# Branch A's background steps: 16 beside its first pair of heads, 10 beside each later one

## The chip, the cores and the metric

The kernel runs on one core of one Trainium2 chip. The metric is the device time of one execution in microseconds (us). The engines are named as the profile names them: PE is TensorE (PEld its weight loads), DVE is VectorE, ACT is ScalarE, POOL is GpSimd, SP is SyncE.

## The reference

One inference step of a trunk of two layers on 1152 tokens (128 of context, 1024 latent), 9 tiles of 128, with 1024 channels. Each layer projects the normed stream by one matrix and feeds three branches from it:

```python
def mixer_tail(x, gate, oa, g_a, ob, g_b, oc, g_c, merge, P):
    m = jax.nn.sigmoid(merge).reshape(B, T, N_BRANCH, D_MODEL)
    y = (m[:, :, 0] * ((oa * jax.nn.silu(g_a)) @ P['w_br_a'])
         + m[:, :, 1] * ((ob * jax.nn.silu(g_b)) @ P['w_br_b'])
         + m[:, :, 2] * ((oc * jax.nn.silu(g_c)) @ P['w_br_c']))
    return x + gate * (y @ P['w_out'])
```

Branch A (oa) is windowed attention of 8 heads with two key heads: each tile of 128 latent queries sees the context block, its own block and its two neighbours, with a sink in the softmax, normed and rotated q and k. Branch B (ob) is a gated linear recurrence over a convolution, branch C (oc) differential attention of 4 heads over all tokens. Each output is multiplied by its own silu gate, which is again a projection of the stream.

## The kernel before, in words

Nearly all matmuls split float32 operands in a high and a low half: `mm3` (L180 to L183) issues three matmuls, high by high, high by low and low by high. A projection of 384 columns over the 1024 channels is 8 times 3 = 24 matmuls of 128x384 into one PSUM bank of the ring ps_s, which has four. PSUM holds besides three banks ps_t (transposes) and one ps_o (outputs).

`unit_phase` does one layer's attention. In the foreground run the heads of branch C and then four pairs of heads of branch A (`g` = 0 to 3), each in five groups of tiles, GR = (0), (1, 2), (3, 4), (5, 6), (7, 8). For a group `q_conv` splits q, `a_probs` makes the scores on PE (L661, L662), adds the mask on DVE (L667, L664 for tile 0), takes exponentials on ACT (L676) and normalises; `flush` then runs the products of the group before (`a_pv`: transposes L701, the high half PT copied by ACT, the low half by DVE L93, products L710 into ps_o, which ACT and DVE copy out into Oa). Foreground code is under `fg`, which gives it a higher priority in the scheduler.

The background is a generator of steps, each one projection chunk of 24 matmuls with what reads it. For branch A 45 steps are left: 9 of `a_gemm2` (q of the later pairs: two tiles at a time through `qk_rows`, L378 to L420), then for each pair three gate chunks (`gate_silu`) and, behind the second to fourth gate and at the end, six steps of the recurrence's projections. `step(n)` takes n of them; the tables BGQ, BG0 and BGA say how many after each group. What is left after the last group runs behind the two last flushes. The order on each engine comes from a scheduler that takes these calls with their priorities.

Two pieces of it matter. `qk_rows` copies two tiles' chunks into `qkraw` (ACT), squares them into `qktmp` (ACT, L388), sums them (DVE, L389), takes an inverse root (DVE, many small `rsq`), multiplies (DVE), and lets POOL scale and rotate them (`qkraw`, `qktmp`, `aq`). `gate_silu` takes a tanh of each chunk (ACT, L449, tile `gt`) and multiplies by the chunk in PSUM (DVE, L102, tile `gate`), which frees the ps_s bank. `qkraw`, `qktmp` and `gt` share the ring D of three buffers in SBUF; RINGS lists the buffers of each ring (W holds weights: `wsraw`, `wsh`, `wsl`, the low half `wsl` made by POOL; T holds PT).

After branch A comes the tail, whose first matmuls write background-like chunks into ps_s and ps_o and start the recurrence (`luhl` into ps_t).

Of the kernel before, what the change touches and what calls it, by code (L numbers as in the profile page):

```python
# [38 lines left out]

BGQ = (2, 2, 2, 3, 2, 1)  # L40
BG0 = (6, 2, 2, 1, 1, 0)
BGA = (3, 2, 2, 2, 2, 2)

RINGS = {"S": 26, "P": 7, "T": 2, "Q": 2, "W": 7, "D": 3, "E": 2, "cx": 1, "tab": 1}

# [9 lines left out]
def hybrid_dit_kernel(ctx, tc, I, O):  # L55
# [30 lines left out]
    def dma(out, in_):  # L86
        nc.sync.dma_start(out=out, in_=in_)
# [262 lines left out]
    def load_wu(L, groups, early=False):  # L350

        src = I["w_in"][L.l].rearrange("(k p) n -> p k n", p=128)
        raws, w = [], []

        def conv(raw):
            m = raw.shape[1]
            hi, lo = al("W", "uwh", m, 384), al("W", "uwl", m, 384)
            split(hi, lo, raw, "A", "P")
            return [(hi[:, j, :], lo[:, j, :]) for j in range(m)]
        for k0 in (0, 3, 6):  # L360
            m = min(3, KT - k0)
            raw = al("W", "wuraw", m, 384)
            for g, c0 in enumerate(groups):
                dma(raw[:, :, 128 * g:128 * g + 128], src[:, k0:k0 + m, c0:c0 + 128])
            raws.append(raw)
            if not early:
                w += conv(raws.pop())
        for raw in raws:
            w += conv(raw)
        return w  # L370
# [72 lines left out]
    def gate_silu(L, c0, put):  # L443

        gate = al("S", "gate", NTOK)

        def f(c, p):
            t = al("D", "gt", 384)
            A.activation(out=t, in_=p, func=AF.Tanh, scale=0.5)  # L449
            stt(gate[:, c * 384:(c + 1) * 384], t, 1.0, p, ALU.add, ALU.mult)  # L450
        hi, lo = ws_load(w_in_cols(L.l, c0), KT)
        put(gate)
        for c in range(3):
            f(c, ws_chunk(L, hi, lo, c))
            yield
# [5 lines left out]
    def c_groups(h):  # L461
        return [CQC + 128 * h, CKC + 128 * h, CVC + 128 * h]

    def qkv_gemm(L, u, w, gains, okey, oval, eng=None):

        u.q, u.kr, u.vr = al("S", "uq", 9, 2, 64), al("S", "ukr", 9, 2, 64), al("S", "uvr", 9, 128)
        for i0 in range(0, 9, 3):
            pss = []
            for t in range(3):
                p = tok_gemm(L, i0 + t, w)  # L470
                acopy(u.vr[:, i0 + t, :], p[:, 256:384])
                pss.append(p)
                if t < 2:
                    yield
            ii = slice(i0, i0 + 3)
            qk_rows(L, i0, pss, gains, [u.q[:, ii, :, :], u.kr[:, ii, :, :]], eng)
            if i0 == 0:
                dma(okey, u.kr[:, 0, :, :])
                dma(oval, u.vr[:, 0, :])
            yield  # L480
# [148 lines left out]
    def a_gemm2(L):  # L629
        u, w = L.ua, L.wu2  # L630
        u.qs = [u.q] + [al("S", "aq", 9, 2, 64) for _ in range(3)]
        for i0 in range(0, 9, 2):
            n = min(2, 9 - i0)
            pss = []
            for t in range(n):
                pss.append(tok_gemm(L, i0 + t, w))
                if t < n - 1:
                    yield
            qk_rows(L, i0, pss, (2, 2, 2), [u.qs[g][:, i0:i0 + n, :, :] for g in (1, 2, 3)])
            yield  # L640
# [86 lines left out]
    def unit_phase(L):  # L727

        l = L.l
        a_groups = [CQA, CKA, CVA]  # L730
        pend = None

        done = None

        def flush():
            nonlocal pend, done
            d, done = done, None
            if pend:
                pend()
                pend = None  # L740
            if d:
                d()

        def start(h):
            u = Unit()
            if h < 4:
                L.units.append(u)
                return qkv_gemm(L, u, L.wu, (0, 1), O["nck"][0, l, :, h, :, :], O["ncv"][0, l, :, h, :],
                                V if h == 0 else None)
            L.ua = u  # L750
            return qkv_gemm(L, u, L.wu, (2, 3), O["nak"][0, l], O["nav"][0, l].rearrange("t v d -> t (v d)"))

        def background():

            for h in range(4):
                L.wu = load_wu(L, c_groups(h + 1) if h < 3 else a_groups)
                yield from start(h + 1)
                yield from gate_silu(L, CGC + 128 * h, lambda gate, u=L.units[h]: setattr(u, "gate", gate))
            L.wu2 = load_wu(L, [CQA + 128, CQA + 256, CQA + 384])
            yield from a_gemm2(L)  # L760
            for g in range(4):
                yield from gate_silu(L, CGA + 128 * g, L.gates.append)
                if g:
                    yield from lru_x(L, g - 1)
            yield from lru_x(L, 3)

        def step(n):
            for _ in range(n):
                next(bg, None)

        def fg(f, *args):
            with tc.high_priority(offset=HPO):
                return f(*args)
        for _ in start(0):
            pass
        bg = background()
        step(BG0[0])
        fg(c_kconv, L, L.units[0], 0)
        for h in range(4):
            u = L.units[h]  # L780
            u.l0 = tl("l0", 9, bufs=2)
            qn = BGQ if h else BG0
            if h:
                step(qn[0])
            fg(v_conv, u, I["cache_c_v"][0, l, :, h, :])
            for g, tiles in enumerate(GR):
                n = len(tiles)
                q = fg(q_conv, u.q[:, tiles[0]:tiles[0] + n, :, :].rearrange("p t m d -> p (t m) d"), 2 * n)
                Ps = [fg(c_probs, L, u, tiles[0], q, 0)]
                fg(flush)  # L790
                if n == 2:
                    Ps.append(fg(c_probs, L, u, tiles[1], q, 1))

                def pend(u=u, tiles=tiles, Ps=Ps, h=h, g=g):
                    if g == 0:
                        u.o = al("P", "O", 1152)
                    c_pv(L, u, tiles, Ps)
                    if g == 4:
                        nonlocal done
                        done = lambda: c_finish(L, u, h)  # L800
                    if g == 1 and h:
                        c_factor(L.units[h - 1], h - 1)
                step(qn[g + 1])
            if h < 3:
                fg(c_kconv, L, L.units[h + 1], h + 1)
            else:
                fg(a_kconv, L)
        u = L.ua
        fg(v_conv, u, I["cache_a_v"][0, l].rearrange("t v d -> t (v d)"), True)
        fg(flush)  # L810
        L.mask = al("P", "mask", 9, 128)
        dma(L.mask, I["mask"].rearrange("p (a b) -> p a b", a=9))
        step(BGA[0])
        for g in range(4):
            if g == 1:
                c_factor(L.units[3], 3)
            for n, tiles in enumerate(GR):
                i, m = tiles[0], len(tiles)
                q = fg(q_conv, (u.qs[g] if g else u.q)[:, i:i + m, :, :].rearrange("p t h d -> p (t h) d"), 2 * m)
                Ps = fg(a_probs, L, g, tiles, q)  # L820
                fg(flush)

                def pend(g=g, n=n, tiles=tiles, Ps=Ps):
                    if n == 0:
                        L.Oa = al("P", "Oa", 1152)
                    a_pv(L, g, tiles, Ps, L.Oa)
                    if n == 4:
                        nonlocal done
                        done = lambda o=L.Oa: a_finish(L, g, o)
                step(BGA[n + 1])  # L830
        fg(flush)
        fg(flush)
        for _ in bg:
            pass


    def lru_x(L, ct):

        def fx(c, p):
            t = al("D", "xt", 384)  # L840
            acopy(t, p)
            dma(xsp[ct][:, 384 * c:384 * c + 384], t)
        def fg(c, p):
            d = al("D", "gxt", 2, 384)
            t, g = d[:, 0], d[:, 1]
            A.activation(out=t, in_=p, func=AF.Tanh, scale=0.5)
            stt(g, t, 1.0, p, ALU.add, ALU.mult)
            dma(gsp[ct][:, 384 * c:384 * c + 384], g)

        for f, c0 in ((fx, CXB), (fg, CGB)):  # L850
            hi, lo = ws_load(w_in_cols(L.l, c0 + 128 * ct), KT)
            for c in range(3):
                f(c, ws_chunk(L, hi, lo, c))
                yield
# [407 lines left out]
    for n, b0 in enumerate((0, 8, 4, 12)):  # L1262
        g = mod_rows(L.D, b0, 4)
# [101 lines left out]
```

## Time and profile before

| | |
|---|---|
| median of three runs | 2767.63 us (2765.0 to 2769.83) |
| the profiled execution | 2773.2 us, its span 2771.4 |
| mean granted clock of PE in it | 0.990 |
| busy share PE, PEld, DVE, ACT, POOL | 97%, 92%, 62%, 47%, 39% |
| instructions | 42562 |

The profile is of one execution. Its span is the time from the first instruction to the last; the execution's own time is 1.8 us longer. Busy shares are means over the whole span. A row of the timeline gives the start and the length of an instruction (of several that follow each other: xN) and, in brackets, how long the engine was idle before it and which instruction released it. The clock is the share of full speed granted to PE.

### The profile page before, as it was taken

Reading aid. Unit: us, or ns where it says so; the run is one execution under the profiler, and the core shown is the slowest. Engines: PE = TensorE matmul, PEld = TensorE weight load, DVE = VectorE, ACT = ScalarE, POOL = GpSimd, SP = SyncE. Lnnn points to the kernel's source line nnn. Section 1 sums busy time; section 2 is a strip of 40 time slices with the busy share of each in tenths; the row PEclk is TensorE's granted clock in tenths of the full one; section 3 lists DMA queues with packets and bytes.
Section 4 is the critical chain, followed back from the end, with each engine's and each line's share of the span. In section 5 each row is a group of like instructions: output and inputs, shape, how many; then the busy total and the mean of one; then the engine's idle time right before and its main releaser. Section 6 shows DMA issues by size and latency. Waiting matters only on the chain. (4 is left out here: it accounts for less than half of the span.)

```text
span 2771.4 us, 42562 instructions
## 1 busy us (share of the span) xinstructions
PE 2681.6 (97%) x15581; PEld 2543.1 (92%) x15581; DVE 1722.8 (62%) x4321; ACT 1292.8 (47%) x2576; POOL 1074.5 (39%) x1368
## 2 busy tenths in 40 slices
PE   7999999989999999999999999999999999999999
PEld 3988998989999989999889999998899999899987
DVE  4797888775664557665367887887666455432242
ACT  4465555656645644122154655656566555511210
POOL 1253454452135555232405354454321465532240
PEclk9999999999999999999999999999999999999999
DMA  6011011111333235544521011111113233432242
GB/s 237 27 34 30 25 34 35 35 44 60 100 106 105 84 130 191 185 139 123 175 70 43 17 35 31 32 42 32 44 57 119 97 96 112 137 124 90 71 143 88
DMA packets 250525, 234.15 MB, mean 84 GB/s; under 512 B 40538, under 2 KB 213964, under 8 KB 250316
## 3 DMA queue, kind: packets, MB, share of 16 engines
q1 hardware_dynamic: 250316, 231.43, 26.3%
q8 instruction: 123, 2.02, 0.3%
q14 instruction: 86, 0.70, 0.1%
HBM read 178.07 MB, written 53.31 MB: 83 GB/s over the span
## 5 line engine op out<-in xcount | busy, mean ns | idle before, releaser
L181 PE MATMUL ps_s<-h,wsh 128*128 128x384 f32 x1440 | 492.7, 342 | 1.0 <-ACT wsh L90 1.0
L182 PE MATMUL ps_s<-h,wsh 128*128 128x384 f32 x1440 | 490.6, 341 | 0.0
L183 PE MATMUL ps_s<-h,wsl 128*128 128x384 f32 x1440 | 490.4, 341 | 0.0
L93 POOL TENSOR_TENSOR wsl<-wsraw,wsh 128x256 fp32r<-128x256 f32 x320 | 262.4, 851 | 307.7 <-ACT wsh L90 223.3
L181 PEld LDWEIGHTS ps_s<-h,wsh 128*128 128x128 f32 x1440 | 272.3, 189 | 2.5 <-ACT wsh L90 1.4
L182 PEld LDWEIGHTS ps_s<-h,wsh 128*128 128x128 f32 x1440 | 272.0, 189 | 0.6
L183 PEld LDWEIGHTS ps_s<-h,wsl 128*128 128x128 f32 x1440 | 271.9, 189 | 0.5
L93 POOL TENSOR_TENSOR qkraw<-qkraw,tab 128x384 f32<-128x384 f32 (+2 forms) x92 | 135.3, 1481 | 276.6 <-DVE qkraw L93 114.6
L538 DVE TENSOR_SCALAR_CACHE_REDUCE P<-ps_s 128x384 f32<-128x384 f32 (+1 forms) x400 | 203.5, 539 | 59.9 <-PE ps_s L537 58.3
L90 ACT ACTIVATE PT<-ps_t 128x512 fp32r<-128x512 f32 (+2 forms) x304 | 161.4, 546 | 143.9 <-PE ps_o L183 76.4
L181 PE MATMUL ps_s<-uwh,h 128*128 128x384 f32 x648 | 221.4, 344 | 1.9 <-ACT h L90 1.9
L182 PE MATMUL ps_s<-uwl,h 128*128 128x384 f32 x648 | 221.5, 343 | 0.8 <-POOL uwl L93 0.8
L93 DVE TENSOR_TENSOR PT<-ps_t,PT 128x512 fp32r<-128x512 f32 (+2 forms) x304 | 187.2, 625 | 53.5 <-ACT PT L90 52.5
L183 PE MATMUL ps_s<-uwh,h 128*128 128x384 f32 x648 | 219.4, 346 | 0.0
L1046 ACT ACTIVATE mg<-ps_s 128x384 f32<-128x384 f32 x144 | 69.7, 484 | 267.4 <-DVE ps_o L102 110.7
L93 POOL TENSOR_TENSOR uwl<-wuraw,uwh 128x256 fp32r<-128x256 f32 x192 | 120.9, 664 | 181.2 <-ACT uwh L90 164.1
L548 ACT ACTIVATE P<-P,csm 128x1152 f32<-128x1152 f32 (+1 forms) x144 | 165.7, 1155 | 50.9 <-DVE csm L97 50.9
L93 POOL TENSOR_TENSOR wb<-wbraw,wb 128x256 fp32r<-128x256 f32 x96 | 81.4, 868 | 268.8 <-ACT wb L90 268.6
L181 PE MATMUL ps_s<-yh,wsh 128*128 128x384 f32 x480 | 165.6, 345 | 0.6 <-DVE asm L667 0.3
L183 PE MATMUL ps_s<-yh,wsl 128*128 128x384 f32 x480 | 164.4, 343 | 0.0
L182 PE MATMUL ps_s<-yl,wsh 128*128 128x384 f32 x480 | 164.3, 342 | 0.0
L536 PE MATMUL ps_s<-ck,qhl 128*128 128x384 f32 x384 | 137.3, 366 | 7.3 <-DVE P L538 6.8
(283 smaller groups left out, 7129.5 us busy)
## 6 DMA issues: line engine op xcount, KB each, us to landing
wsraw<-in_w_in_dram SPq DMA_DIRECT2D x80, 512.0 KB
ysp<-yr SPq DMA_DIRECT2D x32, 576.0 KB
yr<-ysp SPq DMA_DIRECT2D x32, 576.0 KB
wuraw<-in_w_in_dram SPq DMA_DIRECT2D x72, 192.0 KB
ol<-osp SPq DMA_DIRECT2D x24, 576.0 KB
modw<-in_mod_w_dram SPq DMA_DIRECT2D x20, 576.0 KB
modw<-in_mod_w_dram SPq DMA_DIRECT2D x16, 512.0 KB
woraw<-in_w_out_dram SPq DMA_DIRECT2D x16, 512.0 KB
```

What stands on the lines that cost most here:

```text
L90: A.activation(out=out, in_=in_, func=AF.Copy, scale=scale)
L93: e.tensor_tensor(out=out, in0=a, in1=b, op=op)
L181: T.matmul(out=out, lhsT=r(lh), rhs=r(rh), start=first, stop=False)
L182: T.matmul(out=out, lhsT=r(lh), rhs=r(rl), start=False, stop=False)
L183: newest[0] = T.matmul(out=out, lhsT=r(ll), rhs=r(rh), start=False, stop=last)
L536: T.matmul(out=p, lhsT=qh, rhs=kk, start=True, stop=False)
L538: V.tensor_scalar(out=S[:, n * c:n * c + n], in0=p, scalar1=1.0, scalar2=NEG, op0=ALU.mult, op1=ALU.max, accum_out=mx[:, mp, c:c + 1])
L548: A.activation(out=Ss[mp][:, 0:n], in_=Ss[mp][:, 0:n], func=AF.Exp, scale=0.125, bias=nm[:, mp:mp + 1], accum_out=acc)
L1046: A.activation(out=m, in_=p, func=AF.Tanh, scale=0.5)
```

## The change

The table BGA gets two rows: the first for pair 0, the second for the later pairs. The first number of a row, taken once ahead of the loop before, is now taken at the head of each pair. Pair 0 has 5 + 3 + 3 + 2 + 2 + 1 = 16 steps where it had 3 + 5 x 2 = 13, each later pair 2 + 2 + 2 + 2 + 1 + 1 = 10 where it had 5 x 2 = 10. Of the 45 steps the last pair gets the 9 that are left, and none is left for the end, where there were 2.

```diff
--- before.py
+++ after.py
@@ -39,7 +39,7 @@
 
 BGQ = (2, 2, 2, 3, 2, 1)
 BG0 = (6, 2, 2, 1, 1, 0)
-BGA = (3, 2, 2, 2, 2, 2)
+BGA = ((5, 3, 3, 2, 2, 1), (2, 2, 2, 2, 1, 1))
 
 RINGS = {"S": 26, "P": 7, "T": 2, "Q": 2, "W": 7, "D": 3, "E": 2, "cx": 1, "tab": 1}
 
@@ -810,8 +810,8 @@
         fg(flush)
         L.mask = al("P", "mask", 9, 128)
         dma(L.mask, I["mask"].rearrange("p (a b) -> p a b", a=9))
-        step(BGA[0])
         for g in range(4):
+            step(BGA[min(g, 1)][0])
             if g == 1:
                 c_factor(L.units[3], 3)
             for n, tiles in enumerate(GR):
@@ -827,7 +827,7 @@
                     if n == 4:
                         nonlocal done
                         done = lambda o=L.Oa: a_finish(L, g, o)
-                step(BGA[n + 1])
+                step(BGA[min(g, 1)][n + 1])
         fg(flush)
         fg(flush)
         for _ in bg:
```

The scheduler turns this into other orders on the engines. In layer 0, ACT's rows around the four gates (`gt`, the tanh) stood before as follows, `Oa` being the output of the groups of pair 0, `ps_o` the bank of tiles (7, 8), and `PA_6695` the exponentials of pair 1's first scores:

```order
L90 ACTIVATE Oa_6043<-ps_o_6714 64x256 [waits PE_49]
L388 ACTIVATE qktmp_6313<-qkraw_6312 128x384 [waits Pool_49]
L90 ACTIVATE Oa_6043<-ps_o_6714 64x256 [waits DVE_49]
L449 ACTIVATE gt_6472<-ps_s_6447 128x384
L449 ACTIVATE gt_6500<-ps_s_6475 128x384 [waits DVE_49]
L449 ACTIVATE gt_6625<-ps_s_6600 128x384 [waits DVE_49]
L449 ACTIVATE gt_6663<-ps_s_6638 128x384 [waits DVE_49]
L676 ACTIVATE PA_6695,asm_6694<-PA_6695,asm_6694 128x128 [waits DVE_49]
```

and stand now as follows, where `ps_o_6516` holds tiles (3, 4) of pair 0 and `PA_6484` the exponentials of its tiles (5, 6):

```order
L90 ACTIVATE Oa_6180<-ps_o_6516 64x256 [waits PE_49]
L90 ACTIVATE Oa_6180<-ps_o_6516 64x256 [waits DVE_49]
L388 ACTIVATE qktmp_6220<-qkraw_6219 128x384 [waits Pool_49]
L449 ACTIVATE gt_6282<-ps_s_6257 128x384
L449 ACTIVATE gt_6310<-ps_s_6285 128x384 [waits DVE_49]
L449 ACTIVATE gt_6431<-ps_s_6406 128x384 [waits DVE_49]
L449 ACTIVATE gt_6469<-ps_s_6444 128x384 [waits DVE_49]
L676 ACTIVATE PA_6484,asm_6483<-PA_6484,asm_6483 128x512 [waits DVE_49]
```

The four tanhs stand behind the same squares (L388), which wait for POOL; the group ahead of them is now (3, 4) and not (7, 8).

On PE the place is that of the scores behind these gates. Before, the first scores of pair 1 (`xkv`, the context's keys), behind the last products of tiles (7, 8):

```order
L710 MATMUL ps_o_6714<-PT_6754,uv_5632 128x256 [waits Activation_49]
L710 MATMUL ps_o_6714<-PT_6754,uv_5632 128x256 [waits DVE_49]
L661 MATMUL ps_s_6696<-xkv_5627,qhl_6688 128x128 [waits DVE_49]
L662 MATMUL ps_s_6696<-xkv_5627,qhl_6688 128x128
L661 MATMUL ps_s_6700<-xkv_5627,qhl_6688 128x128 [waits DVE_49]
L662 MATMUL ps_s_6700<-xkv_5627,qhl_6688 128x128
L181 MATMUL ps_s_6763<-h_299,wsh_6631 128x384 [waits DVE_49]
L182 MATMUL ps_s_6763<-h_300,wsh_6631 128x384
```

Now the scores of tiles (5, 6) of pair 0, behind the products of (3, 4):

```order
L710 MATMUL ps_o_6516<-PT_6558,uv_5632 128x256 [waits Activation_49]
L710 MATMUL ps_o_6516<-PT_6558,uv_5632 128x256 [waits DVE_49]
L710 MATMUL ps_o_6516<-PT_6558,uv_5632 128x256 x2
L661 MATMUL ps_s_6485<-ak_5572,qhl_6475 128x512 [waits DVE_49]
L662 MATMUL ps_s_6485<-ak_5572,qhl_6475 128x512
L661 MATMUL ps_s_6489<-ak_5572,qhl_6475 128x512 [waits DVE_49]
L662 MATMUL ps_s_6489<-ak_5572,qhl_6475 128x512
L661 MATMUL ps_s_6494<-ak_5572,qhl_6475 128x512 [waits DVE_49]
L662 MATMUL ps_s_6494<-ak_5572,qhl_6475 128x512
L661 MATMUL ps_s_6498<-ak_5572,qhl_6475 128x512 [waits DVE_49]
L662 MATMUL ps_s_6498<-ak_5572,qhl_6475 128x512
L181 MATMUL ps_s_6569<-h_299,wsh_6437 128x384 [waits DVE_49]
```

Where two pairs of small scores waited for DVE and a background chunk (`ps_s_6763`) followed, four pairs of 128x512 wait for DVE, and the background chunk comes behind them. Ahead of the products of (3, 4) stand 48 background rows, and then, from the transposes on, none.

The third place is the end of branch A in layer 0, on PE: the last products of tiles (7, 8) of pair 3. Before, background rows of the tail (`ps_s_9175`) followed, 31 in all:

```order
L710 MATMUL ps_o_8908<-PT_8948,uv_5633 128x256 [waits Activation_49]
L710 MATMUL ps_o_8908<-PT_8948,uv_5633 128x256 [waits DVE_49]
L182 MATMUL ps_s_9175<-h_306,wsh_9092 128x384
L183 MATMUL ps_s_9175<-h_305,wsl_9093 128x384
L181 MATMUL ps_s_9175<-h_307,wsh_9092 128x384
L182 MATMUL ps_s_9175<-h_308,wsh_9092 128x384
```

Now the tail's first product into ps_o (`ps_o_9201`) follows at once:

```order
L710 MATMUL ps_o_8966<-PT_8996,uv_5633 128x256 [waits DVE_49]
L710 MATMUL ps_o_8966<-PT_8996,uv_5633 128x256 x2
L710 MATMUL ps_o_8966<-PT_9006,uv_5633 128x256 [waits Activation_49]
L710 MATMUL ps_o_8966<-PT_9006,uv_5633 128x256 [waits DVE_49]
L181 MATMUL ps_o_9201<-oh_9019,wb_9101 128x384 [waits DVE_49,PE_49]
L182 MATMUL ps_o_9201<-ol_9020,wb_9101 128x384
```

Background rows of `ps_s_9175` stand ahead of the last transposes now, and of the background two rows are left between those transposes and the products.

## Rows read from the trace of the kernel before

**Rows 1.** The page, part 1: busy us (share of the span) and instructions.
```profile
PE 2681.6 (97%) x15581; PEld 2543.1 (92%) x15581; DVE 1722.8 (62%) x4321; ACT 1292.8 (47%) x2576; POOL 1074.5 (39%) x1368
```

**Rows 2.** Windows: stretch, length, busy of PE, PEld, DVE, ACT, POOL; PEclk, DMA.
```profile
560.00:600.00 40.00, 33.77 (x202) 31.31 (x202) 32.95 (x90) 22.87 (x53) 24.29 (x30) 0.96 0.10 27
...
600.00:640.00 40.00, 40.00 (x242) 38.81 (x242) 22.09 (x76) 22.70 (x57) 11.27 (x17) 0.99 0.20 62
...
800.00:840.00 40.00, 38.15 (x225) 37.53 (x224) 13.44 (x24) 14.22 (x27) 13.78 (x20) 1.00 0.36 119
...
1940.00:1980.00 40.00, 35.03 (x194) 33.62 (x193) 28.29 (x101) 22.62 (x58) 21.37 (x27) 0.91 0.12 35
```

**Rows 3.** Waits of PE, layer 0, 480 to 840: us, times, longest.
```profile
PE ps_s L661 <- DVE gate L102: 4.2, 2, 2.7
PE ps_o L710 <- DVE PT L93: 2.3, 4, 1.6
PE ps_o L182 <- DVE PT L93: 1.6, 2, 0.9
...
PE ps_t L181 <- ACT luhl L90: 1.0, 1, 1.0
...
PE ps_t L182 <- POOL luhl L93: 0.9, 1, 0.9
```

**Rows 4.** Waits of PE, the same stretch of layer 1, 1860 to 2220.
```profile
PE ps_s L661 <- DVE gate L102: 2.7, 1, 2.7
...
PE ps_s L661 <- DVE PA L664: 1.1, 1, 1.1
```

**Rows 5.** Timeline of PE, layer 0: start, us, instruction, [idle before <-releaser].
```profile
588.95 0.39 PE L710 MATMUL ps_o<-PT,uv 128*128 128x256 f32 x1 [0.64 <-ACT PT L90]
...
589.67 0.74 PE L710 MATMUL ps_o<-PT,uv 128*128 128x256 f32 x4 [0.34 <-DVE PT L93]
...
591.70 0.86 PE L710 MATMUL ps_o<-PT,uv 128*128 128x256 f32 x5 [0.17 <-DVE PT L93]
...
595.28 0.33 PE L661 MATMUL ps_s<-xkv,qhl 128*128 128x128 f32 x1 [2.72 <-DVE gate L102]
...
597.20 0.48 PE L661 MATMUL ps_s<-xkv,qhl 128*128 128x128 f32 x1 [1.49 <-DVE gate L102]
```

**Rows 6.** Timeline of POOL, layer 0, the rows of q (qk_rows).
```profile
537.49 1.84 POOL L93 TENSOR_TENSOR qkraw<-qkraw,tab 128x768 f32<-128x768 f32 x1 [12.95 <-DVE qkraw L93]
...
544.05 2.12 POOL L93 TENSOR_TENSOR aq<-qkraw,qktmp 128x256 f32<-128x256 f32 x3
...
590.63 2.11 POOL L93 TENSOR_TENSOR aq<-qkraw,qktmp 128x256 f32<-128x256 f32 x3
```

**Rows 7.** Timeline of DVE, layer 0, before and during PE's wait.
```profile
572.65 0.69 DVE L667 CUSTOM_DVE_ANT_0 PA<-ps_s,mask 128x512 f32<-128x512 f32 x1
...
584.93 0.68 DVE L93 TENSOR_TENSOR PT<-ps_t,PT 128x512 fp32r<-128x512 f32 x1
...
594.67 0.56 DVE L102 SCALAR_TENSOR_TENSOR gate<-gt,ps_s 128x384 f32<-128x384 f32 x1
...
596.60 0.55 DVE L102 SCALAR_TENSOR_TENSOR gate<-gt,ps_s 128x384 f32<-128x384 f32 x1
...
597.35 0.98 DVE L93 TENSOR_TENSOR rsq<-rsq 128x6 f32<-128x6 f32 x2
...
598.91 0.24 DVE L93 TENSOR_TENSOR rsq<-rsq 128x6 f32<-128x6 f32 x2
```

**Rows 8.** Timeline of PE, layer 0, scores of a later group.
```profile
778.70 0.79 PE L661 MATMUL ps_s<-ak,qhl 128*128 128x512 f32 x3
```

**Rows 9.** Windows of 5 us, layer 1, behind PE's wait.
```profile
1960.00:1965.00 5.00, 5.00 (x17) 4.96 (x17) 4.81 (x28) 1.84 (x8) 2.05 (x3) 0.50 0.25 97
```

**Rows 10.** Timeline of PE and DVE, layer 0, the end of branch A.
```profile
811.73 0.76 PE L710 MATMUL ps_o<-PT,uv 128*128 128x256 f32 x5
...
813.79 0.43 DVE L102 SCALAR_TENSOR_TENSOR Oa<-ps_o,Oa 64x256 f32<-64x256 f32 x1 [0.44 <-ACT Oa L90]
```

## Prediction

> **What bounds the kernel now.** I read the page first: TensorE is busy 2681.6 us of the span [rows 1], so about 90 us are idle, and the other engines matter only where TensorE waits for them. The windows show where that is in a layer. From 600 us on branch A leaves no gap (40.00 busy of 40), while the stretch before it, 560 to 600, has 33.77, and the same place of layer 1, 1940 to 1980, 35.03 at a granted clock of 0.91 [rows 2]. So a step that moves from the later heads to the first saves nothing where it leaves: the later heads were full. What is gained or lost lies in the short gaps around the first pair of heads and at the end of the branch. The waits of TensorE name these gaps: scores (L661) behind VectorE's gate product, 4.2 us in layer 0 [rows 3], 2.7 in layer 1 with 1.1 behind a mask step right after it [rows 4]; branch C's last products behind the low half of P transposed (ps_o L182, 1.6); A's own products behind the same (L710, 2.3, of which one is 1.6); the recurrence's first matmuls behind luhl (1.0 + 0.9) [rows 3].
>
> The largest is the one to understand. At 592.56 TensorE has ended the products of tiles (7, 8) and wants a ps_s bank for the first scores of pair 1; all four hold chunks of a gate, and it waits 2.72 and then 1.49 [rows 5]. The chunks were multiplied long ago. What is late is their reader: ScalarE's tanh stands behind the squares of the last q rows, whose buffer (three in ring D) POOL frees only at 592.74, when it ends the fourth pair of q tiles [rows 6]. The first gate product ends at 595.23, the next 1.93 later [rows 7]. So the stall is the end of a chain: VectorE's multiply of the q rows, POOL's rotation, tanh, gate product, bank.
>
> **The change, term by term.** No arithmetic is added or removed; the 45 background steps of a layer stand elsewhere. 16 stand beside pair 0 instead of 13, 10 beside each of the next two as before, 9 beside the last instead of 10, and the two that ran after the last flush are gone from there.
>
> *The gate stall.* In the new order the four tanhs still stand behind the same squares, but now ahead of the scores of tiles (5, 6) of pair 0. The chain gets no shorter; call Q the end of VectorE's multiply of the fourth pair. POOL needs 8.68 from there when nothing else is between (537.49 to 546.17) [rows 6]. The first gate ended 2.49 after POOL's last q row before; VectorE had output copies ahead of it there, so I take 2.1, and the gate ends at Q + 10.8. TensorE cannot use the time: its order has no background row between the transposes of (3, 4) and the scores. VectorE's low half of the transposed P, 0.68 [rows 7], now stands behind that multiply, so the products start at Q + 0.7 and take 3.6, as they did from 588.95 to 592.56 [rows 5]. TensorE stands at the scores at Q + 4.3 and waits 6.5. Bounds: 4.7 if the gate follows POOL by 1.2 (its own 0.56 and about as much for the tanh) and the products take 0.9 longer; 7.4 if it follows by 2.49 and the products lose their gaps of 0.34 and 0.17.
>
> Then the second difference. Before, two gates were waited for, by small scores; now four pairs of 128x512 scores take all four banks. The gates were 1.93 apart. VectorE's rsq steps between them took 0.98 for two while POOL multiplied an output block, 0.24 when it did not, and POOL's order there now has one such block instead of three; against that a mask step of 0.69 comes between two gates [rows 7]. I take 1.7; the ends are 1.9 and 1.25 (product and mask step alone). A pair of scores hides some 0.5 of it (three such matmuls took 0.79) [rows 8], so three gates cost 3 x 1.2 = 3.6 (2.2 to 4.2). The stall is 10.1 per layer against 4.2 and 3.8: **+5.9 and +6.3**.
>
> On those rsq steps the Trainium skill, page "SBUF — State Buffer", section "SBUF: two separate sides", says that a VectorE instruction with two inputs in SBUF and a GpSimd instruction that reads SBUF take one pair of ports in turn, the second waiting out the whole of the first. The 0.98 against 0.24 agrees. By that rule alone, with two of three blocks gone, the spacing would be near the lower end, and the sum some 2.5 us lower over both layers.
>
> *The products behind the multiply.* They waited 0.64 + 0.34 + 0.17 in their old order [rows 5]; behind the chain of the fourth pair they may wait for more than that: **+0.6** per layer (0 to 1.5).
>
> *The clock.* After the old stall the granted clock was 0.50 from 1960 to 1965 in layer 1, so 2.5 us of work were lost there [rows 9]; in layer 0 it was 0.96 over 40 us, some 1.6 [rows 2]. A longer stall with a few scores in it will lose about as much: **+0.5** (0 to 2.9).
>
> *The end of branch A.* Before, 20 and 19 background rows covered the last transposes' copies, and 31 the copies out of the only ps_o bank. Now two rows are left ahead of the last products and none behind. The products then show their bare gaps, 0.64 + 0.34 + 0.17 = 1.15 [rows 5]. The tail's first product into ps_o waits for the copies, which took from the last product's end at 812.49 to 814.22, 1.73 [rows 10]. The luhl gaps right behind, 1.9 in all [rows 3], have that much more time to close, of which I count 0.4. Together **+2.5** per layer (1 to 4).
>
> *Gains.* Nine, five, seven and eight background rows now stand among branch C's last products, where TensorE waited 1.6: **-1.6** (0 to -1.6). The 1.6 ahead of A's products of (1, 2) is partly filled by the moved steps: **-0.8** (0 to -1.6) [rows 3].
>
> Sum: 5.9 + 0.6 + 0.5 + 2.5 - 1.6 - 0.8 = 7.1 in layer 0 and 7.5 in layer 1, **+14.6**. The profiled execution took 2773.2, so its sum is 2787.8; it was 5.6 above the median of the runs shown, 2767.63, and against that the time is **2782**. With all the low bounds (a stall of 6.9) the layers come to 0.5 and 0.9 and the time to 2769; with the high ones (a stall of 11.6) to 15.8 and 16.2, 2800.
>
> **Rivals.** *The stall goes.* If Q comes 6.5 us further ahead of TensorE than I place it, the first wait is covered, and at 10 us all four are. For it: the q tiles' matmuls do stand earlier now, and an order has no times in it. Against it: VectorE's order has the fourth pair's whole chain behind the softmax of (3, 4) and ahead of that group's transposed P, so TensorE cannot fall behind it by more than those products. Then -4.2 and -3.8 of waits, -1.6 and -2.5 of clock, and -1.6 - 0.8 + 2.5 in each layer: -11.9, **2756**, faster.
>
> *The stall moves and keeps its size.* If only the first gate is late, by 2.7 as before, and the other three come under the mask steps, it is a wash and 0.6 + 2.5 - 1.6 - 0.8 = 0.7 a layer are left: **2769**, the same.
>
> *The end of A costs the clock too.* The clock fell to a half after 3.8 us of waits with little work between [rows 4, 9]. The end of A has now some 3 us of them, in pieces. If the clock falls there as well, 2.5 a layer come on top: **2787**. The Trainium skill, page "TensorE: Matmul & The Clock Gate", section "A second HAM failure mode: psum-queue depth-cycling", tells of a kernel whose short idles between groups of matmuls brought the clock down again and again; no run here shows that yet. Against it: the luhl gaps of 1.9 in all left the clock at 1.00 from 800 to 840 [rows 2].
>
> **How the numbers follow.** A measurement of this kernel can tell about 0.2%, 5.5 us, from no change. The forecast has 0.53 and the rival on the clock at the end 0.18; both lie above that, so slower has 0.71. The stall that moves has 0.13, the same. The stall that goes has 0.16, faster. The range is 2760 to 2798: it leaves out most of the faster case and the uppermost end of the forecast's own 2769 to 2800.
>
> **What would show it.** Right: in the profile after, the wait of L661 for the gate product is gone where pair 1 begins and stands, some 10 us in several pieces, ahead of the scores of (5, 6) of pair 0, in both layers; the windows behind it are full; ps_o L182 no longer waits for PT in branch C's last products; and at the end of A the tail's first product waits for the Oa copies. Wrong: if that L661 wait is under 4 us a layer, the banks were not held by the chain of q rows; if the end of A has no gap over 1 us, its term was invented.

## The result and the profile after

The changed kernel takes **2792.35 us** (median of four runs, 2791.08 to 2796.36); the kernel before, run beside it on the same chip, 2768.73 (2765.0 to 2772.77). The ratio is 1.0088, its 95% interval 1.0075 to 1.0101. The change costs 23.6 us; 14.6 were predicted, 2782 with a range of 2760 to 2798. Direction and place were right, the size was 9 short. Two disturbed executions are left out of all that follows: one of 3268.65 us in the sixth experiment and one of 5716.86 of the kernel before, run beside several.

The profiled execution took 2796.36, 23.2 more than the profiled one of before. The page first, part 1 (busy us, share of the span, instructions), the row that answers to [rows 1]:

```profile
PE 2689.8 (96%) x15581; PEld 2548.1 (91%) x15581; DVE 1720.3 (62%) x4321; ACT 1290.8 (46%) x2576; POOL 1076.1 (39%) x1368
```

The work is the same to the instruction. PE is busy 8.2 us longer with it, which is a lower clock, and the rest of the 23 is idle time. The windows tell where (stretch, length, busy of PE, PEld, DVE, ACT, POOL, then PEclk, DMA share, GB/s). The kernel before at 720 to 760, then the change:

```profile
720.00:760.00 40.00, 40.00 (x254) 39.24 (x252) 23.13 (x68) 25.85 (x67) 8.58 (x11) 1.00 0.30 96
```
```profile
560.00:600.00 40.00, 30.89 (x170) 27.93 (x169) 27.30 (x90) 20.96 (x49) 19.45 (x25) 0.87 0.06 14
...
720.00:760.00 40.00, 38.46 (x240) 37.56 (x240) 23.02 (x65) 23.88 (x59) 6.88 (x9) 0.96 0.13 42
800.00:840.00 40.00, 34.47 (x180) 32.28 (x179) 23.99 (x40) 20.04 (x37) 17.33 (x20) 0.87 0.28 93
1940.00:1980.00 40.00, 31.06 (x172) 28.41 (x173) 28.86 (x94) 20.56 (x45) 19.46 (x25) 0.87 0.07 15
```

Against [rows 2] the stretch of the stall lost 2.9 us of busy time and the clock fell from 0.96 to 0.87; that was forecast. The end of the branch, 800 to 840, lost 3.7 and its clock went from 1.00 to 0.87; 2.5 of loss was forecast there, and none by the clock. At 720 to 760, which the prediction held to be full, 1.5 of busy time is gone and the clock fell to 0.96. The waits of PE in layer 0, 480 to 860 (us in total, times, longest), answer to [rows 3]:

```profile
PE ps_s L661 <- DVE gate L102: 6.3, 2, 5.6
PE ps_o L181 <- DVE Oa L102: 3.1, 1, 3.1
PE ps_o L710 <- DVE PT L93: 2.9, 5, 1.1
PE ps_s L661 <- ACT qhl L90: 2.1, 2, 1.5
PE ps_s L181 <- ACT qkraw L90: 1.3, 1, 1.3
PE ps_s L181 <- ACT oh L90: 1.1, 1, 1.1
```

The wait of ps_o L182 for PT is gone, 1.6 as forecast, and so are those for luhl. The gate wait grew from 4.2 to 6.3, and four rows are new: Oa at the end of A, qkraw ahead of the stall, oh at the end, and qhl in the middle of the later pairs. Layer 1 has the same list.

Where the stall stands now, in PE's timeline (start, length, instruction, idle before it and its releaser):

```profile
568.58 0.38 PE L710 MATMUL ps_o<-PT,uv 128*128 128x256 f32 x1 [0.36 <-ACT PT L90]
569.72 0.74 PE L710 MATMUL ps_o<-PT,uv 128*128 128x256 f32 x4 [0.76 <-DVE PT L93]
...
572.88 0.62 PE L710 MATMUL ps_o<-PT,uv 128*128 128x256 f32 x3 [0.40 <-DVE PT L93]
579.06 0.80 PE L661 MATMUL ps_s<-ak,qhl 128*128 128x512 f32 x1 [5.56 <-DVE gate L102]
...
580.99 0.80 PE L661 MATMUL ps_s<-ak,qhl 128*128 128x512 f32 x1 [0.71 <-DVE gate L102]
...
582.01 0.63 PE L661 MATMUL ps_s<-ak,qhl 128*128 128x512 f32 x1
...
583.72 0.52 PE L181 MATMUL ps_s<-h,wsh 128*128 128x384 f32 x1
```

This is the forecast place: products of (3, 4), then scores of (5, 6) of pair 0 behind gates. PE stops at 573.50 and reaches its next chunk at 583.72. The chain behind it, from VectorE's multiply on, on DVE, POOL, ACT and DVE in turn:

```profile
567.98 0.96 DVE L93 TENSOR_TENSOR qkraw<-qkraw,rsq 128x768 f32<-128x768 f32 x1
```
```profile
569.02 1.83 POOL L93 TENSOR_TENSOR qkraw<-qkraw,tab 128x768 f32<-128x768 f32 x1 [2.81 <-DVE qkraw L93]
...
575.20 2.08 POOL L93 TENSOR_TENSOR aq<-qkraw,qktmp 128x256 f32<-128x256 f32 x3
579.09 1.00 POOL L93 TENSOR_TENSOR Oa<-Oa,gate 128x384 f32<-128x384 f32 x1 [1.80 <-DVE rsq L99]
```
```profile
577.32 0.52 ACT L388 ACTIVATE qktmp<-qkraw 128x384 f32<-128x384 f32 x1 [2.53 <-POOL aq L93]
577.75 0.47 ACT L449 ACTIVATE gt<-ps_s 128x384 f32<-128x384 f32 x1
```
```profile
578.46 0.55 DVE L102 SCALAR_TENSOR_TENSOR gate<-gt,ps_s 128x384 f32<-128x384 f32 x1
...
579.12 1.21 DVE L97 TENSOR_SCALAR rsq<-rsq 128x6 int32<-128x6 int32 x4
580.25 0.23 DVE L99 TENSOR_SCALAR rsq<-rsq 128x6 int32<-128x6 int32 x2
580.40 0.54 DVE L102 SCALAR_TENSOR_TENSOR gate<-gt,ps_s 128x384 f32<-128x384 f32 x1
...
581.78 0.54 DVE L102 SCALAR_TENSOR_TENSOR gate<-gt,ps_s 128x384 f32<-128x384 f32 x1
...
583.16 0.54 DVE L102 SCALAR_TENSOR_TENSOR gate<-gt,ps_s 128x384 f32<-128x384 f32 x1
```

POOL ends its fourth pair at 577.28, ACT starts the last square at once, the first tanh follows, the first gate ends at 579.01 and PE at 579.06 takes the bank. What the rows leave open is whether the rest of the loss hangs on this stall or is a thing of its own.

### The profile page after: what moved, and what is told of

The parts are those of the page before. It is cut to its first block, busy times and chain, and to the rows that moved or that the text cites. A ratio compares the mean times of both kernels' runs of the same rounds, so it can differ in the third digit from the quotient of the medians.

```text
span 2793.7 us, 42546 instructions
## 1 busy us (share of the span) xinstructions
PE 2689.8 (96%) x15581; PEld 2548.1 (91%) x15581; DVE 1720.3 (62%) x4321; ACT 1290.8 (46%) x2576; POOL 1076.1 (39%) x1368
## 4 chain that ended last, share of the span: by engine, by line
PE 44%; DVE 5%; ACT 1%; issue 1%; DMA 1%; POOL 1%; SPq 0%; ACTq 0%; DVEq 0%; POOLq 0%
PE ps_s L181 11%; PE ps_s L182 11%; PE ps_s L183 11%; PE ps_o L182 1%; PE ps_o L181 1%; PE ps_o L183 1%; PE ps_t L565 1%; PE ps_s L536 1%; PE ps_s L537 1%; DVE P L538 1%; PE ps_o L710 1%; PE ps_t L701 1%; DVE P L102 1%; PE ps_s L661 0%; DVE PT L93 0%
## 5 line engine op out<-in xcount | busy, mean ns | idle before, releaser
L182 PE MATMUL ps_s<-h,wsh 128*128 128x384 f32 x1440 | 490.6, 341 | 0.0
L182 PEld LDWEIGHTS ps_s<-h,wsh 128*128 128x128 f32 x1440 | 271.9, 189 | 0.9
L182 PE MATMUL ps_s<-uwl,h 128*128 128x384 f32 x648 | 220.5, 341 | 0.8 <-POOL uwl L93 0.8
L182 PE MATMUL ps_s<-yl,wsh 128*128 128x384 f32 x480 | 164.4, 342 | 0.0
```

Source lines behind the costliest of these rows:

```text
L182: T.matmul(out=out, lhsT=r(lh), rhs=r(rl), start=False, stop=False)
```

## The experiments

Each was timed beside the kernel before. A diff is against the changed kernel where nothing else is said, and shows the changed lines alone. The letters of the theories hold within one expectation: each names its own.

**1. Pair 0's steps alone.** The later pairs keep their even row.

```diff
-BGA = ((5, 3, 3, 2, 2, 1), (2, 2, 2, 2, 1, 1))
+BGA = ((5, 3, 3, 2, 2, 1), (0, 2, 2, 2, 2, 2))
```

> Pair 0 keeps its 16 steps (5 ahead, 3, 3, 2, 2, 1), the later pairs go back to no step at their head and 2 behind each group. Theory A (the gate stall of pair 0 and the bare end of branch A cost most, each with the clock it takes down): the stall ahead of the scores of (5, 6) stays (5.6 + 0.7 of waits in each layer), and the end of A stays bare, since the order still puts no background row behind the last products; only the waits for qhl in pairs 1 and 2 (2.5 us a layer, with the half clock that follows the longer one) go. That gives 4 to 8 us less than after: 2784 to 2788. Theory B (the steps at the heads of the later pairs, which rearrange pairs 1 to 3, cost most): within 4 us of before, 2765 to 2773.

Measured: 2776.25, ratio to before 1.0033 (1.0022 to 1.0044). It lies between the two expectations, and neither held: pair 0's 16 steps cost 9 us, and 0.55% of the time, some 15 us, comes only with the later rows. Its waits of PE in layer 0:

```profile
PE ps_s L661 <- DVE gate L102: 6.3, 2, 5.6
...
PE ps_o L181 <- DVE Oa L102: 1.9, 1, 1.9
```

The stall is here in full; the waits for qhl and oh are gone, and that for Oa is 1.9 instead of 3.1; 1.2 in three pieces behind the mask sums (asm) is new.

**2. The later pairs' rows alone.**

```diff
-BGA = ((5, 3, 3, 2, 2, 1), (2, 2, 2, 2, 1, 1))
+BGA = ((3, 2, 2, 2, 2, 2), (2, 2, 2, 2, 1, 1))
```

> Pair 0 goes back to 13 steps (3 ahead, 2 behind each group); the later pairs keep the changed row (2 at the head, 2, 2, 2, 1, 1). Two steps are left for the end, and the order has background rows among and behind the last products again. Theory A, additive (the later rows cost what the changed table lost beyond e1_first_only, 16 us, wherever they stand): 2780 to 2786. Theory B (they cost it only together with pair 0, because 16 + 10 + 10 use the steps up and leave the end of A bare): no wait of ps_o for the Oa copies, the wait for qhl of some 2 us a layer at most, 2767 to 2773.

Measured: 2772.97, ratio 1.0021 (1.0011 to 1.0031), some 6 us over before, at the upper end of what theory B allowed. Alone the two halves cost 9 and 6, together 24: the price of a row depends on the other row. Here 13 + 30 = 43 steps are taken, so two are left behind the last products, and no wait for Oa shows; with 16 steps beside pair 0 all 45 are taken.

**3. The tanh out of ring D.** It is written into the gate's own tile, in place of a buffer that the q rows' squares use too. Nothing else moves by intent.

```diff
-            t = al("D", "gt", 384)
+            t = gate[:, c * 384:(c + 1) * 384]
...
-            stt(gate[:, c * 384:(c + 1) * 384], t, 1.0, p, ALU.add, ALU.mult)
+            stt(t, t, 1.0, p, ALU.add, ALU.mult)
```

> The changed table; the tanh of a gate chunk is written into the gate's own buffer instead of a buffer of ring D, and the product is made in place. Theory A (four gates wait for GpSimd's q rows because tanh shares ring D with them): the wait of L661 for the gate product falls from 6.3 a layer to under 1.5, the half clock behind it goes, and the time falls by 10 to 16 from after: 2776 to 2782. The end of A stays as it is. Rival (what is late is VectorE, busy with the inverse roots and the softmax, not the ring): the gates come no earlier, L661 still waits over 4 us a layer, and the time stays within 4 us of after.

Measured: 2768.75, ratio 1.0008 (0.9999 to 1.0018): the whole price of the change, 22 us by the two ratios, more than theory A asked. Its waits of PE in layer 0:

```profile
PE ps_o L181 <- DVE Oa L102: 3.2, 1, 3.2
...
PE ps_s L661 <- ACT qhl L90: 2.0, 2, 1.4
PE ps_s L181 <- ACT oh L90: 1.1, 1, 1.1
```

No score waits for a gate any more, while the waits at the end and in the middle of the branch are as long as before the edit. So the gate stall is the ring, as the prediction had it, and those waits do not hang on the stall.

**4. The same edit on the kernel before.**

> The table of before with the tanh written into the gate's own buffer. Theory A: the wait of L661 where pair 1 begins (4.2 us in layer 0, 3.8 in layer 1) goes and with it most of the half clock behind it (1.6 and 2.9): 8 to 12 us less than before, 2757 to 2761. Rival (the ring is not what is late): within 3 us of before.

Measured: 2756.56, ratio 0.9961 (0.9946 to 0.9975), 10.3 us faster than before. The old stall at the head of pair 1 was the same head-of-line wait, and its window answers to [rows 2]:

```profile
560.00:600.00 40.00, 37.20 (x232) 35.02 (x231) 35.92 (x108) 21.07 (x51) 20.19 (x24) 1.00 0.13 34
```

**5. Pair 0's steps alone, with the tanh in place:** edits 1 and 3 together.

> Pair 0's 16 steps with the later pairs as before (the table of e1_first_only), and the tanh written into the gate's own buffer. Theory A (of e1_first_only's loss the gate stall is the whole, and what the table gains in branch C's last products remains): the stall of 6.3 us a layer and its half clock go, 16 to 22 us less than e1_first_only, 2754 to 2760, about what the table of before gives with the same edit. Rival (the bare end of A and the q rows, not the gates, are what pair 0's steps cost): 2764 to 2770.

Measured: 2756.5, ratio 0.9956 (0.9942 to 0.9971). It ties with the fourth, and both beat the two kernels of this case. Ratios to the kernel before, side by side:

| | tanh in ring D | tanh in place |
|---|---|---|
| rows of before | 1 | 0.9961 |
| pair 0 has 16, the others an even row | 1.0033 | 0.9956 |
| pair 0 has 16, the others the row of the change | 1.0088 | 1.0008 |

Read down: with ring D, pair 0's 16 steps cost 0.33%; without it nothing that can be told. The row of the later pairs costs 0.55% in one column and 0.52% in the other, so its price does not hang on the stall. Nor does it hang on the waits for qhl. The fifth has the even row and is cheap, and in layer 0 it waits for them almost as long as the third (2.0):

```profile
PE ps_s L661 <- ACT qhl L90: 1.9, 2, 1.5
```

**6. PE kept busy at the stall.** Ahead of the scores of (5, 6) of pair 0 PE gets 44 transposes whose result nothing reads.

```diff
+        if (g, tiles[0]) == (0, 3):
+            fill = ps("t", 4, 128)
+            for f in range(44):
+                T.transpose(fill[:, f % 4, :], th[:, 0, 0:128], ident)
```

> The changed kernel with 44 transposes of 128x128 that nothing reads, behind the products of (3, 4) of pair 0 in each layer, so that TensorE works through most of the 5.6 us in which it waited for the gate. Theory A (the half clock behind the stall comes from the idle time and costs by itself): the granted clock stays at 1.00 there, and the 2.6 us of work that the half clock took in each layer come back, 4 to 6 us less than after, 2786 to 2789. Theory B (the four scores and the next chunk are pinned by the four gates whatever the clock): the clock stays up, but only what ran at half speed behind the fourth gate comes back, 0 to 3 us less than after, 2789 to 2793.

Measured: 2792.77 (2788.58 to 2796.91), ratio 1.0091 (1.0074 to 1.0108). That is what theory B allowed and no gain on the change, but with single times 8 us apart it can't tell a loss of a few us from none. The profile says more. PE's timeline and 5-us windows at the stall:

```profile
577.12 0.50 PE L661 MATMUL ps_s<-ak,qhl 128*128 128x512 f32 x1 [0.88 <-DVE gate L102]
...
579.04 0.80 PE L661 MATMUL ps_s<-ak,qhl 128*128 128x512 f32 x1 [1.19 <-DVE gate L102]
...
581.77 0.52 PE L181 MATMUL ps_s<-h,wsh 128*128 128x384 f32 x1
```
```profile
570.00:575.00 5.00, 5.00 (x46) 5.00 (x47) 2.21 (x4) 1.30 (x4) 4.84 (x7) 1.00 0.01 3
575.00:580.00 5.00, 2.93 (x16) 2.00 (x15) 3.91 (x16) 2.38 (x5) 1.41 (x2) 0.91 0.00 0
580.00:585.00 5.00, 5.00 (x22) 4.61 (x22) 4.99 (x29) 1.98 (x6) 0.00 (x0) 0.75 0.00 2
```

The long wait is filled at a clock of 1.00, and the first pair of scores behind it runs at full clock (0.50 a row where the change has 0.80). Yet nothing is gained up to the next chunk: from the first score to the second pair it is 1.92 (577.12 to 579.04) against 1.93 in the change (579.06 to 580.99), and from there to the next chunk 2.73 in both. VectorE's second gate sets the first distance, so theory B was right there: half a clock on that pair cost nothing.

Behind the second wait the clock is at half in this kernel too, so the run doesn't show what full clock would give on the last three pairs. The change's own rows bound it. Four pairs of scores and the next chunk take the five banks that come free first, and VectorE, busy without a break from 580 to 585, frees them with the gates that end at 579.01, 580.94 and 582.32 and with two mask steps between:

```profile
581.01 0.67 DVE L667 CUSTOM_DVE_ANT_0 PA<-ps_s,mask 128x512 f32<-128x512 f32 x1
...
582.40 0.67 DVE L667 CUSTOM_DVE_ANT_0 PA<-ps_s,mask 128x512 f32<-128x512 f32 x1
```

The fifth bank is free at 583.07, and the chunk starts at 583.72: at full clock it could come 0.65 earlier at most.

**7. The tail's first product into a ps_s bank,** so that it needn't wait for the Oa copies.

```diff
-        p2 = ps("so"[(j + c) % 2], 384)
+        p2 = ps("s" if (order, j, c) == (0, 0, 1) else "so"[(j + c) % 2], 384)
```

> The changed table; the tail's first product that went into the one ps_o bank goes into a ps_s bank. Theory A (behind the last products of A the tail waits for the copies out of the only ps_o bank): the waits of 3.1 and 3.0 us go, and the half clock behind them (2.2 us a layer) with them; since the luhl waits of before may come back (up to 1.9 a layer), 4 to 10 us less than after, 2782 to 2788. Rival (the end of A is short of work in any order, and the wait only moves to a ps_s bank or to luhl): within 3 us of after.

Measured: 2800.79, ratio 1.0122 (1.0107 to 1.0138): 8.4 slower than the change. Neither expectation held. The wait for Oa is gone, and a longer one is in its place. PE's timeline, then ACT's:

```profile
837.95 0.69 PE L181 MATMUL ps_t<-luhl,gw 128*128 128x384 f32 x1 [9.72 <-ACT luhl L90]
```
```profile
831.74 1.35 ACT L876 ACTIVATE lu<-lx,cols 128x1152 f32<-128x1152 f32 x1 [2.17 <-DMA lx<-xsp]
837.38 1.55 ACT L90 ACTIVATE luhl<-lu 128x384 fp32r<-128x384 f32 x3 [4.29 <-DVE lu L102]
```

The recurrence's load lx takes a buffer of ring T, which PT holds, and everything up to luhl follows it. PE's last product of A ends at 827.90 and luhl comes 10 us later. In the change the tail's first product and a chunk stand behind the last products and cover that time; here they were spent ahead of them. Up to the first luhl matmul the two profiled executions are level, 360.8 us against 361.0 from the transposes of P named below. The 200 matmuls from there on take 38.3 instead of 35.3, at a clock of 0.68 from 840 to 845 where the change has 1.00.

**8. Two steps left behind the last pair.**

```diff
-BGA = ((5, 3, 3, 2, 2, 1), (2, 2, 2, 2, 1, 1))
+BGA = ((5, 3, 3, 2, 2, 1), (2, 2, 2, 2, 1, 1), (2, 2, 2, 2, 1, 1), (2, 2, 2, 1, 0, 0))
...
-            step(BGA[min(g, 1)][0])
+            step(BGA[g][0])
...
-                step(BGA[min(g, 1)][n + 1])
+                step(BGA[g][n + 1])
```

> The changed table, but the last pair has 7 steps (2, 2, 2, 1, 0, 0), so that two steps are left for the end as before the change. Theory A (it is the two missing steps that leave the end bare): the waits for ps_o and for oh go, 8 us or more less than after, 2782 to 2785. Theory B (the scheduler spends left-over steps ahead of the last products anyway, as its order does here, so the number left does not matter): the wait of ps_o for the Oa copies stays at 1.7 us or more, and the time stays within 5 us of after.

Measured: 2788.5, ratio 1.0082 (1.0066 to 1.0099), by the intervals not to be told from the change's 1.0088. Theory B held: the wait for Oa is 1.9, as in the first experiment, and that for oh is gone, yet the time is not back.

**9 and 10. Which number of the later row is dear?** In the ninth the last number goes, in the tenth the first.

```diff
-BGA = ((5, 3, 3, 2, 2, 1), (2, 2, 2, 2, 1, 1))
+BGA = ((5, 3, 3, 2, 2, 1), (2, 2, 2, 2, 2, 0))
```

> Pair 0 as in the change; each later pair keeps the 2 steps at its head but has 2, 2, 2, 2, 0 behind its groups instead of 2, 2, 2, 1, 1. Theory H (what the later rows cost comes from the steps at the head of a pair, which stand ahead of its first q and scores and leave fewer behind the softmax): the waits for qhl and for oh stay, and the time is within 4 us of after, 2788 to 2796. Theory T (it comes from the single steps behind the last two groups): those waits change, and the time is within 4 us of e1_first_only, 2772 to 2780.

```diff
-BGA = ((5, 3, 3, 2, 2, 1), (2, 2, 2, 2, 1, 1))
+BGA = ((5, 3, 3, 2, 2, 1), (0, 3, 3, 2, 1, 1))
```

> Pair 0 as in the change; each later pair has no step at its head and 3, 3, 2, 1, 1 behind its groups, so the single steps behind the last two stay. Theory H: the waits for qhl and for oh go, and the time is within 4 us of e1_first_only, 2772 to 2780. Theory T: they stay, and the time is within 4 us of after, 2788 to 2796.

Measured: 2793.03, ratio 1.0087 (1.007 to 1.0105), and 2791.42, ratio 1.0083 (1.0066 to 1.0099). Both theories fall in the form they had: neither the steps at the head nor the short tail alone carries the price. In layer 0 of the ninth the waits for qhl are gone, in the tenth they stand (2.5); in both that for oh is gone and that for Oa is 1.9, and the products wait longer for the high half of P transposed (ACT PT, 3.3 and 2.5 where the change has 0.7). Of the settings tried for the later pairs beside pair 0's 16 steps, only the even one is cheap.

## Why the prediction came out as it did

**The stall: mechanism right, too large.** Its place and its releaser came as told, in both layers, and the experiments on the tanh show the cause both ways. The steps, with Q the end of VectorE's multiply at 568.94: products end at Q + 4.6 (4.3 predicted), first gate at Q + 10.1 (10.8). The first wait was 5.6 instead of 6.5. The second term was the larger miss, "three gates cost 3 x 1.2 = 3.6": only one more gate was waited for, 0.7. The third was not, because a mask step frees the first pair's bank ahead of it, and the gates came 1.94, 1.38 and 1.38 apart against 1.7 three times. The rsq steps took 1.21 for four beside POOL's one block of Oa (579.09 to 580.09) and 0.23 for two afterwards, which left the last two distances to a mask step, a gate product and what of rsq doesn't overlap them. The Trainium skill, page "SBUF — State Buffer", section "SBUF: two separate sides", says that a GpSimd instruction takes a pair of ports in turn with a VectorE one that has two inputs in SBUF or runs in a two-port mode. The 1.21 against 0.23 agrees with the turns, though these four steps have one input each and no row shows their mode. By that rule the spacing was to be near the lower bound of 1.25, as two of three were: the sum should have followed it. So the waits grew by 2.1 in layer 0, and eight scores at half clock, 0.43 apart instead of some 0.21, took 1.7 more (of which full clock would give back at most 0.65, by the sixth experiment): 3.8 in place of 5.9. Another 1.3 was not counted: a chunk ahead of the stall waits for the copy into qkraw, which needs the same ring.

**Products, gains: right.** The products' gaps were 0.36 + 0.76 + 0.40, 0.4 over [rows 5] (0.6 predicted). The drain of C gave its 1.6, and the wait of 1.6 ahead of (1, 2) fell to 1.07 (0.5 of the predicted 0.8).

**The step that failed: "a step that moves from the later heads to the first saves nothing where it leaves", and therefore costs nothing there.** The later pairs were full because their steps stood where they did. With the change, scores of a later pair wait for ACT's qhl, PE's timeline:

```profile
659.15 0.91 PE L661 MATMUL ps_s<-ak,qhl 128*128 128x512 f32 x3 [0.58 <-ACT qhl L90]
...
726.62 1.08 PE L661 MATMUL ps_s<-ak,qhl 128*128 128x512 f32 x4 [1.54 <-ACT qhl L90]
```

On ACT the copy of 725.99 stands behind four exponentials of the group before. Together with a gap of 0.35 behind PT that is 2.5 in layer 0, where nothing was counted. The table of ratios shows the size of the whole: with either form of the tanh the later row costs over 0.5%, some 15 us, most of what the change cost, and the prediction had it at nothing. That the time lies in the range is in part luck: by the first experiment pair 0's steps alone, from which nearly all its terms came, cost 9 us where the sum had 14.6.

**The end of A: the mechanism right, short by a copy.** The tail's first product does wait for Oa, but 3.1 instead of 1.73, since ACT makes a weight's high half first:

```profile
826.01 1.06 ACT L90 ACTIVATE wsh<-wsraw 128x1024 fp32r<-128x1024 f32 x1 [1.33 <-DMA wsraw<-in_w_in_dram]
827.09 0.38 ACT L90 ACTIVATE Oa<-ps_o 64x256 f32<-64x256 f32 x1
```

The products' bare gaps were 0.34 + 0.34 where 1.15 was taken, and waits for oh and ol, 1.08 + 0.43, were not seen at all. Less the 1.9 of luhl, which closed fully, that is +3.4 against 2.5.

**The clock: 0.5 taken, several us come.** The rival that gave the end of A the clock too (2787, chance 0.18) had this right, and not far enough. 5-us windows of the change, layer 0:

```profile
725.00:730.00 5.00, 3.46 (x15) 2.89 (x15) 4.15 (x10) 4.07 (x10) 0.00 (x0) 0.83 0.11 41
...
810.00:815.00 5.00, 3.25 (x12) 2.16 (x11) 3.25 (x6) 3.49 (x9) 2.52 (x4) 0.86 0.00 0
815.00:820.00 5.00, 5.00 (x27) 5.00 (x27) 1.40 (x5) 1.34 (x2) 0.00 (x0) 0.80 0.01 3
825.00:830.00 5.00, 1.90 (x8) 1.73 (x9) 1.10 (x3) 2.21 (x4) 1.00 (x1) 0.73 0.74 256
830.00:835.00 5.00, 5.00 (x19) 5.00 (x19) 3.78 (x8) 0.94 (x1) 0.00 (x0) 0.59 0.71 244
```

Busy time by one less the clock, these and the window behind 726 (730 to 735, busy 5.00 at 0.83) give 0.6 + 0.9 + 0.5 + 1.0 + 0.5 + 2.1 = 5.6 us, where the kernel before had a clock of 1.00 at the end [rows 2]. No row shows beside them what else would have held PE, so I count the loss there in full, unlike in the stall. Behind the wait of 1.54 a run bears that out, as said below; at the end of A it is argued. The kernel before lost 1.5 behind its stall (596.56 to 601.56), which the change has no more: +4.1 net. The Trainium skill, page "TensorE: Matmul & The Clock Gate", section "A second HAM failure mode: psum-queue depth-cycling", told of a clock brought down by short idles again and again. The trace agrees: it fell three times behind waits of 1.54, of 1.08 + 0.43 and of 3.10, with work between. But it does not fall each time. The eighth experiment has the first of these waits too, and its clock stayed up:

```profile
726.70 1.09 PE L661 MATMUL ps_s<-ak,qhl 128*128 128x512 f32 x4 [1.53 <-ACT qhl L90]
```
```profile
725.00:730.00 5.00, 3.47 (x22) 2.87 (x21) 4.08 (x10) 4.14 (x10) 0.00 (x0) 1.00 0.11 41
```

PE's order from there on is the same in both kernels, and the first 48 matmuls take 7.81 us in the eighth experiment and 9.36 in the change: the 1.5 counted for this drop are lost indeed, and only in an execution that has the drop.

The sum in layer 0 is 3.8 + 1.3 + 0.4 − 1.6 − 0.5 + 2.5 + 3.4 + 4.1 = 13.4. From the transposes of P that both kernels share ahead of the changed place (484.06 before, 478.79 after) to the first luhl matmul (828.49, 839.82) the change takes 16.6 longer, so some 3 us are not placed. Over the same stretch layer 1 takes 361.2 instead of 346.0. So the two layers cost more than the 23.2 between the two profiled executions; the rest comes back outside them. The change was 5.3 ahead at that first point already, and that lead is not the change's, since PE's order up to there is the same: the clock was 0.98 from 0 to 480 in the kernel before and 0.99 here. It is 3.6 faster again behind layer 1's first luhl matmul; why, no row here shows.

**What stays open.** Why the later pairs' even row is cheap and three uneven ones are dear was not settled. No single wait carries the price: the ninth has no wait for qhl or oh and only 1.9 for Oa and is as dear as the change, while the fifth has the waits for qhl and is cheap. What goes with the price is the sum of PE's waits in layer 0: with ring D it is 17.9 in the change, 17.7, 17.7 and 18.5 in the eighth to tenth, and 14.0 with the even row; with the tanh in place 10.0 in the third and 6.8 in the fifth. That is 3 to 4 us a layer. The rest is in part the clock: over 480 to 840 it is 0.97 in the change and 0.99 with the even row. Why an uneven row makes PE wait more, whichever wait it is, no run shows.

That the two rows are not additive (9 and 6 alone, 24 together) was measured; that it comes from the two steps which the second experiment leaves for the end is argued from its missing Oa wait and not shown, and the eighth, which left two for the end as well, gained nothing that can be told.

## What to carry to other kernels

When scores wait for a bank, look up what the bank's reader waits for: here a tanh stood behind a square in ScalarE's order because both took buffers of one ring of three, and writing the tanh into its destination gave 10 us on the kernel before and over 20 on the changed one, while no placing of steps that was tried with ring D beat the kernel before. A stretch without gaps is full because of the filler that stands in it: price what leaves it, too. At the end of a phase look at what stands behind the last products: the copies and the next phase's first chain need cover there. Before pricing a lower clock, ask which engine sets the pace: where VectorE did, half clock cost next to nothing here.

## What the runs showed of the hardware

The granted clock fell to its half level behind waits as short as 1.54 us in one piece (726.62 in the change; the same wait in the eighth experiment left it at 1.00), or 0.88 and 1.19 with a pair of scores between (sixth experiment, 0.75 from 580 to 585); the prediction had thought of some 3.8 us of waits with little work between. Half clock on the first pair of scores in a stall that VectorE paces cost nothing (1.93 us to the next pair against 1.92 at full clock), and on all of them at most 0.65 us of some 1.7.
